# The end of the first channel mixer, done in token halves that follow each other

## The chip, the cores and the metric

The kernel runs on one core of a Trainium2 chip. The metric is the device time of one execution in microseconds (us). Three runs took 3246.5, 3255.47 and 3258.47 us, median 3255.47 us. The profiled execution is one more, of 3260.19 us.

Engines are named as in the profile: PE does the matrix products, DVE, ACT and POOL work elementwise on tiles of 128 partitions, SP issues most of the DMAs. Each engine has a queue of its own, and its instructions start in the trace in the order of that queue.

## The reference

A sequence of 1024 tokens with 1024 features, after 16 meta tokens, goes through two blocks. What matters here is the end of the first block, its channel mixer, and the start of the second, in the parts of a recurrent mixer (RWKV) that are projections with a token shift:

```
y = (gelu(conv(rmsnorm(x1, g_pre) @ w_gate)) * (rmsnorm(x1, g_pre) @ w_up)) @ w_down
x2 = x1 + rmsnorm(y, g_post)                     # end of the first block
p = rmsnorm(x2, mix_norm_gain) @ w_in            # second block
p = p + (shift(p) - p) * mix                     # shift: one token back
r, k, v, wd, ad, gd = split(p)                   # 512 columns each for r, k, v
w = w0 + tanh(wd) @ w_lora_up;  a = sigmoid(a0 + ad @ a_lora_up);  g = sigmoid(gd) @ g_lora_up
kk = normalised k * k_k, per head                # "removal"
```

The columns of wd, ad and gd are the "lora" columns: 128 of them in a first projection (l1) and 32 in a second (l2).

## The kernel before, in words

Activations lie with features on partitions: eight tiles (j = 0 to 7) of 128 features by 1024 tokens, worked on in two token halves, columns 0 to 511 and 512 to 1023. Every product is made of three fp32r products (`mm3`, L196 to L198): high by high, high by low and low by high part. So each operand is split: the high part by a rounding copy on ACT, the low part by a subtraction on DVE or POOL.

**The down projection** (`down`) sums over 22 hidden tiles, taken two at a time. For a pair it loads hidden tile and weights and splits both (four tiles `dn` of each tag XH and XL, which hold eight each, so two pairs are there at once). Then for the first token half, and then for the second, and for each j, six matmuls of 512 columns sum the pair in a PSUM bank, and DVE adds the bank to `y` (L149). On the last pair, `each` also feeds the first norm: ACT squares `y`, POOL adds the squares of j = 0 to 6 in `acc`, and PE sums `acc` and the last square over the partitions (`add_sums`, L292, four matmuls of one column that the trace shows as eight records).

**The end of the mixer** (`ffn1`) then makes the inverse root from the sums (`rstd`: thirteen tiny DVE operations, the wide `rdg`, and four PE matmuls at L318 that spread it over the partitions). For each half and each j: a scaling of `y` (DVE, L156), the residual `x1` loaded from DRAM and added (POOL, L149), the high part `xh` (ACT) and the low part `xl` (DVE, L156), the square for the second norm (ACT, and L292 on PE), and a store of the result to `dx2`. A second `rstd` per half gives `rs`, by which later projections are scaled.

**The second block** begins with the weights of the lora products, then `lora_in`: `shifted` for l1, then for l2, each over both token halves: a weight column of `w_in`, 24 matmuls for each half, `p` (DVE, the PSUM bank times `rs`), a difference on POOL and a combination `d` on DVE. Its results go through tanh to DRAM (`dlora`), from where later steps read them. Then come rotary tables, the attention mask, the output gate (bank q), and the twelve projections r, k, v (`rkv`), the four k first (key0 to key3), each of these followed by `removal`: a square on ACT, two matmuls into the one bank c1 (`pc`), logarithm and exponential on ACT, and a chain over DVE and POOL whose scratch tiles lie in tag A, which holds three. In this region two PSUM banks (m0, m1) take the projections.

The order in every engine's queue is fixed when the program is built: a scheduler replays the program with its own durations and places each instruction where it would be free to go. The order of the source is its wish, not its result.

Of the kernel before, what the change touches and what calls it, by code (L numbers as in the profile page):

```python
# [8 lines left out]
F32 = mybir.dt.float32  # L9
# [8 lines left out]
P = 128  # L18
D = 1024
KD = 8  # L20
# [28 lines left out]
class Build:  # L49
# [1102 lines left out]
    def down(self, hid, w_down, y, last, each=None, after=None, between=None):  # L1152
# [14 lines left out]
        for f in range(0, NF, 2):  # L1167
            fs = [load(f), load(f + 1)]
            end = f == NF - 2
            for a, b in last if end else CH2:  # L1170
                for j in range(KD):
                    ps = self.mm_ps([P, b - a])
                    for i, (g, w) in enumerate(fs):
                        self.mm3(ps, (w[0][:, j, :], w[1][:, j, :]), (g[0][:, a:b], g[1][:, a:b]), i == 0, i == 1)
                    if f == 0:
                        nc.scalar.copy(y[j][:, a:b], ps)
                    else:
                        self.tt(y[j][:, a:b], y[j][:, a:b], ps, ALU.add)
                    if each and end:
                        each(j, a, b)  # L1180
                if after and end:
                    after(a, b)
            if between:
                between(f)

    def ffn1(self, fx):
# [18 lines left out]
        self.down(hid, I["w_ffn_down"][0], y, CH2, each)  # L1205
        rp = [self.rstd(tot[a], b - a, D) for a, b in CH2]
        self.rs = self.slot([P, T2], name="rs", tag="R")
        self.xh, self.xl = [], []
        for i, (a, b) in enumerate(CH2):
            tot = self.sums_ps()  # L1210
            for j in range(KD):
                if j % 2 == 0:
                    x1 = self.slot([P, 2, b - a], name="x1", tag="XE")
                    self.dma(out=x1, in_=self.dx1[j:j + 2, :, a:b].rearrange("j p t -> p j t"))
                if i == 0:
                    self.xh.append(self.slot([P, T2], F32R, "xh", "XH"))
                    self.xl.append(self.slot([P, T2], F32R, "xl", "XL"))
                h, l = self.xh[j][:, a:b], self.xl[j][:, a:b]
                t = y[j][:, a:b]
                self.stt(t, t, gp[:, j:j + 1], rp[i], ALU.mult, ALU.mult)  # L1220
                self.tt(t, t, x1[:, j % 2], ALU.add, eng=nc.gpsimd)
                self.act(h, t, AF.Copy, scale=gm[:, j:j + 1])
                self.stt(l, t, gm[:, j:j + 1], h.bitcast(F32), ALU.mult, ALU.subtract)
# [933 lines left out]
```

## Time and profile before

| | |
|---|---|
| median of three runs | 3255.47 us |
| the profiled execution | 3260.19 us |
| its span in the trace | 3258.5 us |
| PE busy | 3022.7 us, 93% |
| DVE / POOL / ACT busy | 62% / 41% / 35% |
| mean granted TensorE clock | 0.939 |

The last matmul of the down projection starts at 1592.87 us of the span and key0 starts at 1658.37 us. The clock that PE was granted is given as a share of the full 2.4 GHz; 0.50 is 1.2 GHz. A matmul that waits for another engine leaves the queue standing; a wait is listed with the engine that ended it. The slower half of a stretch may be due to the clock as well as to waits, so the granted clock stands in each row of a stretch.

### The profile page before, as it was taken

To read this page: it belongs to the slowest core of one execution; us is meant where nothing else is said; L and a number is where in the kernel's file an instruction comes from. 1 tells how busy PE (TensorE), PEld (TensorE's weight loads), DVE (VectorE), ACT (ScalarE), POOL (GpSimd) and SP (SyncE) were. 2 spreads that over 40 slices of the span, in tenths; PEclk is the share of its full clock that TensorE was granted. 3 is DMA by queue.
4 is the path that set the end of the run, shared out by engine and by line. 5 is a ranking of instruction groups with operands and counts; after the bars stand their busy time and mean duration, and the time that the engine had idled before them with its cause. 6 is when DMAs were issued, how large, how long until landed. Compare 5 with 4: busy or idle time off the path is not lost.

```text
span 3258.5 us, 52664 instructions
## 1 busy us (share of the span) xinstructions
PE 3022.7 (93%) x20614; PEld 2686.7 (82%) x20614; DVE 2010.1 (62%) x3618; ACT 1138.8 (35%) x2166; POOL 1337.7 (41%) x1291
## 2 busy tenths in 40 slices
PE   7999999989889999999999988977998899999998
PEld 6899999879789999877877776766787788887777
DVE  6555653774676666466766555557665866664666
ACT  3334323334343333311333323334444433334111
POOL 2777310033664444232532355542204754454430
PEclk9999999889799999999899988858998899999999
DMA  5233631335212222432223554443336122224321
GB/s 132 84 99 102 180 108 47 99 105 144 83 53 84 79 83 81 155 103 73 91 86 134 147 129 113 111 114 109 100 102 207 52 78 84 78 78 170 120 84 52
DMA packets 322535, 336.83 MB, mean 103 GB/s; under 512 B 60081, under 2 KB 270734, under 8 KB 322286
## 3 DMA queue, kind: packets, MB, share of 16 engines
q1 hardware_dynamic: 289168, 310.22, 30.6%
q10 hardware_dynamic: 33118, 23.24, 2.4%
q8 instruction: 162, 2.65, 0.3%
q14 instruction: 87, 0.71, 0.1%
HBM read 232.66 MB, written 96.40 MB: 101 GB/s over the span
## 4 chain that ended last, share of the span: by engine, by line
PE 62%; DVE 11%; POOL 5%; issue 5%; DMA 5%; ACT 2%; SPq 1%; ACTq 0%; DVEq 0%; POOLq 0%
PE pm L196 13%; PE pm L197 13%; PE pm L198 12%; PE px L197 5%; PE px L196 5%; PE px L198 5%; DVE dn L149 2%; PE px L292 1%; POOL Z L149 1%; POOL fs L149 1%; DVE t L149 1%; PE pa L1856 1%; PE pc L1523 1%; SPq L142 1%; DVE y L149 1%
## 5 line engine op out<-in xcount | busy, mean ns | idle before, releaser
L196 PE MATMUL pm<-xh,whi 128*128 128x512 f32 (+5 forms) x1344 | 453.1, 337 | 17.4 <-DVE th L149 14.2
L198 PE MATMUL pm<-xh,wlo 128*128 128x512 f32 (+5 forms) x1344 | 451.4, 336 | 1.0 <-DVE wlo L149 1.0
L197 PE MATMUL pm<-xl,whi 128*128 128x512 f32 (+5 forms) x1344 | 451.9, 336 | 0.0
L149 DVE TENSOR_TENSOR y<-y,pm 128x512 f32<-128x512 f32 (+1 forms) x336 | 218.0, 659 | 159.9 <-PE pm L198 159.6
L196 PEld LDWEIGHTS pm<-xh,whi 128*128 128x128 f32 (+1 forms) x1344 | 261.4, 194 | 40.3 <-DVE th L149 12.5
L196 PE MATMUL pm<-dn,dn 128*128 128x512 f32 (+1 forms) x736 | 285.8, 389 | 6.9 <-DVE y L149 6.4
L197 PE MATMUL pm<-dn,dn 128*128 128x512 f32 (+1 forms) x736 | 282.7, 384 | 0.7 <-POOL dn L149 0.7
L198 PE MATMUL pm<-dn,dn 128*128 128x512 f32 (+1 forms) x736 | 282.6, 384 | 0.0
L198 PEld LDWEIGHTS pm<-xh,wlo 128*128 128x128 f32 (+1 forms) x1344 | 260.8, 194 | 22.0 <-DVE wlo L149 1.4
L197 PEld LDWEIGHTS pm<-xl,whi 128*128 128x128 f32 (+1 forms) x1344 | 261.4, 195 | 19.5 <-issue 0.5
L149 POOL TENSOR_TENSOR dn<-hid,dn 128x1024 fp32r<-128x1024 f32 x44 | 131.7, 3011 | 250.9 <-ACT dn L1160 250.9
L197 PE MATMUL px<-t,sh 128*128 128x258 f32 (+2 forms) x684 | 218.0, 319 | 7.4 <-DVE t L149 7.4
L196 PE MATMUL px<-t,sh 128*128 128x258 f32 (+2 forms) x684 | 216.9, 317 | 1.4 <-DVE gt L149 1.3
L198 PE MATMUL px<-t,sl 128*128 128x258 f32 (+2 forms) x684 | 215.9, 316 | 0.0
L149 DVE TENSOR_TENSOR wlo<-wraw,whi 128x1024 fp32r<-128x1024 f32 (+2 forms) x114 | 157.6, 1384 | 86.3 <-ACT whi L170 80.2
L196 PEld LDWEIGHTS pm<-dn,dn 128*128 128x128 f32 x736 | 138.2, 188 | 44.3 <-DVE y L149 14.4
L170 ACT CAST whi<-wraw 128x1024 fp32r<-128x1024 f32 (+2 forms) x114 | 103.3, 907 | 184.5 <-PE pm L197 153.8
L198 PEld LDWEIGHTS pm<-dn,dn 128*128 128x128 f32 x736 | 138.2, 188 | 29.9
L197 PEld LDWEIGHTS pm<-dn,dn 128*128 128x128 f32 x736 | 138.4, 188 | 29.6 <-POOL dn L149 1.2
L170 ACT CAST dn<-wd 128x1024 fp32r<-128x1024 f32 x44 | 46.1, 1047 | 291.2 <-PE pm L197 290.7
L149 POOL TENSOR_TENSOR wraw<-wraw,par 128x1024 f32<-128x1024 f32 (+1 forms) x36 | 76.0, 2111 | 173.1 <-DMA wraw<-in_w_in_dram 137.5
L197 PEld LDWEIGHTS px<-t,sh 128*128 128x128 f32 x684 | 130.7, 191 | 18.2 <-DVE t L149 9.4
(611 smaller groups left out, 8771.1 us busy)
## 6 DMA issues: line engine op xcount, KB each, us to landing
wraw<-in_w_in_dram SPq DMA_DIRECT2D x61, 512.0 KB
dhid<-up SPq DMA_DIRECT2D x44, 512.0 KB
wd<-in_w_ffn_down_dram SPq DMA_DIRECT2D x44, 512.0 KB
hid<-dhid SPq DMA_DIRECT2D x44, 512.0 KB
wra<-in_w_ffn_up_dram SPq DMA_DIRECT2D x33, 512.0 KB
wrb<-in_w_ffn_up_dram SPq DMA_DIRECT2D x33, 512.0 KB
dg<-th SPq DMA_DIRECT2D x16, 514.0 KB
wraw<-in_w_out_dram SPq DMA_DIRECT2D x16, 512.0 KB
```

What stands on the lines that cost most here:

```text
L142: self.nc.sync.dma_start(out=out, in_=in_)
L149: (eng or self.nc.vector).tensor_tensor(out=o, in0=a, in1=b, op=op)
L170: self.nc.scalar.copy(hi, src)
L196: nc.tensor.matmul(ps, a[0], b[0], start=start, stop=False, **kw)
L197: nc.tensor.matmul(ps, a[0], b[1], start=False, stop=False, **kw)
L198: nc.tensor.matmul(ps, a[1], b[0], start=False, stop=stop, **kw)
L292: self.nc.tensor.matmul(ps[:bw, i:i + 1], src[:, i * bw:i * bw + bw], self.ones[:, 0:1], start=start and i == 0, stop=stop and i == n - 1)
L1523: nc.tensor.matmul(ps[:, h], maps[c][:, h], S[:, h], start=True, stop=True)
L1856: nc.tensor.matmul(self.po[:, i - 4 * ch], pT[:, i * P - a:i * P - a + P], self.vx[j % 2][:, k].rearrange("p e v -> p (e v)")[:, 2 * e:2 * ...
```

## The change

`down` gets a helper `chunk`, and where `each` is given (the first mixer) the last four hidden tiles are kept together: first token half with the first pair, first token half with the second pair, and then the second half with all four in one sum of twelve matmuls per j. The first half's norm, scaling, residual and second sum (`update`, with the residual added by DVE in place of POOL) are written inside `down`, in front of the second half. The splits of the first half come behind `down`, since all XH and XL tiles are taken until its last matmuls; then come the second half's norm, update and split. `shifted` takes several specifications: l1, l2 and key0 are projected together, their three first halves and then their three second halves. The tiles p and d of l1 and l2 lie in tag A and those of key0 in T, the weights of l2 in a small `narrow` tile (tag W). `lora_in` comes ahead of `lora_weights`, and `rkv` takes key0 ready made. Of the diff the new lines stand here; those taken out, but for the residual's add, are in the functions printed above.

```diff
...
+        def chunk(fs, a, b, first, end):
+            for j in range(KD):
+                ps = self.mm_ps([P, b - a])
+                for i, (g, w) in enumerate(fs):
+                    self.mm3(ps, (w[0][:, j, :], w[1][:, j, :]), (g[0][:, a:b], g[1][:, a:b]), i == 0, i == len(fs) - 1)
+                if first:
+                    nc.scalar.copy(y[j][:, a:b], ps)
+                else:
+                    self.tt(y[j][:, a:b], y[j][:, a:b], ps, ALU.add)
+                if each and end:
+                    each(j, a, b)
+            if after and end:
+                after(a, b)
+        joint = 4 if each else 0
+        for f in range(0, NF - joint, 2):
...
+                chunk(fs, a, b, f == 0, end)
...
+        if joint:
+            (a, b), *others = last
+            fs = [load(f) for f in (NF - 4, NF - 3)]
+            chunk(fs, a, b, False, False)
+            more = [load(f) for f in (NF - 2, NF - 1)]
+            chunk(more, a, b, False, True)
+            for a, b in others:
+                chunk(fs + more, a, b, False, True)
...
+        def update(j, a, b, rp, x1, ps):
+            t = y[j][:, a:b]
+            self.stt(t, t, gp[:, j:j + 1], rp, ALU.mult, ALU.mult)
+            self.tt(t, t, x1[:, j % 2], ALU.add)
+            self.square_sum(ps, t, j == 0, j == KD - 1)
+            self.dma(out=self.dx2[j, :, a:b], in_=t)
+        def residual(j, a, b):
+            x1 = self.slot([P, 2, b - a], name="x1", tag="XE")
+            self.dma(out=x1, in_=self.dx1[j:j + 2, :, a:b].rearrange("j p t -> p j t"))
+            return x1
+        def split(j, a, b):
+            h, l, t = self.xh[j][:, a:b], self.xl[j][:, a:b], y[j][:, a:b]
+            self.act(h, t, AF.Copy, scale=gm[:, j:j + 1])
+            self.stt(l, t, gm[:, j:j + 1], h.bitcast(F32), ALU.mult, ALU.subtract)
+        def after(a, b):
+            if a:
+                return
+            rp, ps = self.rstd(tot[a], b - a, D), self.sums_ps()
...
-                self.tt(t, t, x1[:, j % 2], ALU.add, eng=nc.gpsimd)
...
+                    x1 = residual(j, a, b)
+                update(j, a, b, rp, x1, ps)
+            self.rstd(ps, b - a, D, self.rs[:, a:b])
+        self.down(hid, I["w_ffn_down"][0], y, CH2, each, after)
+        self.xh, self.xl = ([self.slot([P, T2], F32R, n, t) for _ in range(KD)] for n, t in (("xh", "XH"), ("xl", "XL")))
+        (a, b), (c, d) = CH2
+        for j in range(KD):
+            split(j, a, b)
+        rp, ps = self.rstd(tot[c], d - c, D), self.sums_ps()
+        for j in range(KD):
+            if j % 2 == 0:
+                x1 = residual(j, c, d)
+            update(j, c, d, rp, x1, ps)
+            split(j, c, d)
+        self.rstd(ps, d - c, D, self.rs[:, c:d])
...
+    def shifted(self, *specs):
+        ws, pp, res = [], [], []
+        for j0, m, _, tag in specs:
+            ws.append(self.wcol(self.I["w_in_2"][0], j0, m) if m == P else self.narrow(self.I["w_in_2"][0], j0, m))
+            pp.append(self.slot([P, T2 + 1], name="p", tag=tag)[:m])
+        for c in CH2:
+            for (j0, m, _, _), w, p in zip(specs, ws, pp):
+                self.proj(w, self.x, [c], lambda ci, a, b, ps: self.tt(p[:, 1 + a:1 + b], ps, self.rs[:m, a:b], ALU.mult), m=m)
+        for (j0, m, mix, tag), p in zip(specs, pp):
+            self.ts(p[:, :1], p[:, 1:2], 0.0, ALU.mult)
+            d = self.slot([P, T2], name="d", tag=tag)[:m]
+            self.tt(d, p[:, :T2], p[:, 1:], ALU.subtract, eng=self.nc.gpsimd)
+            self.stt(d, d, mix, p[:, 1:], ALU.mult, ALU.add)
+            res.append(d)
+        return res
+    def narrow(self, src, c0, m):
+        raw, hi, lo = (self.slot([P, KD, m], dt, "nw", "W") for dt in (F32, F32R, F32R))
+        self.dma(out=raw, in_=src[:, c0:c0 + m].rearrange("(k p) m -> p k m", p=P))
+        self.split_to(hi, lo, raw)
+        return hi, lo
...
+        l1, l2, self.key0 = self.shifted((1536, P, self.par["mix_lora"][:, 0:1], "A"), (1664, 32, self.mixl[:, 0:1], "A"),
+                                         (512, P, self.par["mix"][:, 4:5], "T"))
...
+                if (i, j) == (1, 0):
+                    t = self.key0
+                else:
+                    t, = self.shifted((512 * i + j * P, P, self.par["mix"][:, 4 * i + j:4 * i + j + 1], "T"))
...
+        B.lora_in()
```

What the schedule made of it stands in the order of the queues. In these rows a number behind a name is that of the buffer.

On PE, around l1 in the program before (`pm_2127` and `pm_2128` are the halves of l1, `px_2098` the sums of the second half's second norm, `px_2097` the spread inverse root):

```order
10172 L197 MATMUL pm_2128_16457<-xl_16116,whi_16426 128x512
10173 L198 MATMUL pm_2128_16457<-xh_16115,wlo_16427 128x512
10174 L196 MATMUL pm_2128_16457<-xh_16128,whi_16426 128x512
10175 L197 MATMUL pm_2128_16457<-xl_16129,whi_16426 128x512
10176 L198 MATMUL pm_2128_16457<-xh_16128,wlo_16427 128x512
10177 L292 MATMUL px_2098_16249<-ones_71,sq_16304 128x1 x4
10178 L292 MATMUL px_2098_16249<-ones_71,sq_16315 128x1 x4
10179 L292 MATMUL px_2098_16249<-ones_71,sq_16328 128x1 x4
10180 L318 MATMUL px_2097_16243<-rdg_16241,ones_71 128x128 x4
10181 L292 MATMUL px_2098_16249<-ones_71,sq_16339 128x1 x4
10182 L196 MATMUL pm_2128_16457<-xh_16143,whi_16426 128x512
```

On PE in the changed program, from the end of l1's first half (`pm_2123`) on (`px_2068` the sums of the second half's first norm, `px_2089` its spread root, `px_2090` the sums of its second norm, `pm_2125` key0's and `pm_2124` l2's first half):

```order
10162 L198 MATMUL pm_2123_16413<-xh_16185,wlo_16395 128x512
10163 L292 MATMUL px_2068_16167<-ones_71,acc_14331 128x1 x4
10164 L292 MATMUL px_2068_16167<-ones_71,sq_16172 128x1 x2
10165 L318 MATMUL px_2053_16030<-rdg_16028,ones_71 128x128 x4
10166 L292 MATMUL px_2068_16167<-ones_71,sq_16172 128x1 x2
10167 L318 MATMUL px_2089_16228<-rdg_16226,ones_71 128x128 x4
10168 L292 MATMUL px_2090_16233<-ones_71,sq_16238 128x1 x4
...
10175 L292 MATMUL px_2090_16233<-ones_71,sq_16321 128x1 x4
10176 L196 MATMUL pm_2125_16465<-xh_16178,whi_16408 128x512
...
10182 L196 MATMUL pm_2124_16439<-xh_16178,nw_16400 32x512
```

Before, the matmuls of l1's second half stand between these sums; now all of l1's first half stands ahead of the second half's two norms, and the first halves of key0 and l2 behind both of them. The spread root of the first half's first norm stands 21 matmuls ahead of the end of the down projection.

On ACT in the program before, where the down projection ends (the squares of the second half's first norm, then the first split and the first square of the second norm):

```order
1086 L159 ACTIVATE sq_16032<-y_14328 128x512
1087 L159 ACTIVATE sq_16043<-y_14329 128x512
1088 L159 ACTIVATE sq_16059<-y_14330 128x512
1089 L159 ACTIVATE xh_16115<-y_14323,par_117 128x512
1090 L159 ACTIVATE sq_16121<-y_14323 128x512
```

On ACT in the changed program (up to row 1097 the first half's second norm and split, from 1098 on the squares of the second half's first norm):

```order
1094 L159 ACTIVATE sq_15996<-y_14329 128x512
1095 L159 ACTIVATE xh_16184<-y_14329,par_117 128x512
1096 L159 ACTIVATE sq_16005<-y_14330 128x512
1097 L159 ACTIVATE xh_16185<-y_14330,par_117 128x512
1098 L159 ACTIVATE sq_16065<-y_14324 128x512
1099 L159 ACTIVATE sq_16082<-y_14325 128x512
...
1104 L159 ACTIVATE sq_16172<-y_14330 128x512
```

The squares of the second half's first norm stood ahead of every split; now they stand behind the splits and squares of the first half. On DVE, too, the first half's scalings, adds and splits stand ahead of the second half's first norm, and `p` of l1's first half stands behind all of the second half's scalings, adds and splits.

On PE in the program before, the first two removals (`pc`, two each) with other matmuls between them:

```order
10374 L1361 MATMUL pc_2189_16783<-rm_16779,blk_16386 128x512
10375 L1677 MATMUL pq_2151_16625<-ident_66,mask_16601 128x128 x4
...
10396 L1361 MATMUL pc_2190_16786<-rm_16779,blk_16386 128x512
10397 L196 MATMUL pq_2158_16649<-gd_16646,lg_16640 128x512
...
10473 L1361 MATMUL pc_2201_16865<-rm_16861,blk_16386 128x512
10474 L196 MATMUL pq_2168_16683<-gd_16680,lg_16640 128x512
```

And in the changed program:

```order
10464 L1410 MATMUL pc_2182_16770<-rm_16763,blk_16370 128x512
10465 L196 MATMUL pq_2157_16696<-gd_16693,lg_16687 128x512
...
10506 L1410 MATMUL pc_2193_16849<-rm_16845,blk_16370 128x512
...
10513 L1410 MATMUL pc_2194_16852<-rm_16845,blk_16370 128x512
...
10568 L1410 MATMUL pc_2205_16931<-rm_16927,blk_16370 128x512
10569 L1410 MATMUL pc_2206_16934<-rm_16927,blk_16370 128x512
```

From the second `pc` of the first removal to the first `pc` of the second there were 77 rows and are 42; from there to the third removal there are 55 (70 before, rows 10498 to 10568).

## Rows read from the trace of the kernel before

**Rows 1.** The page: busy time by engine.
```profile
PE 3022.7 (93%) x20614; PEld 2686.7 (82%) x20614; DVE 2010.1 (62%) x3618; ACT 1138.8 (35%) x2166; POOL 1337.7 (41%) x1291
```
**Rows 2.** Windows: stretch, length, busy PE, PEld, DVE, ACT, POOL, clock, DMA, GB/s.
```profile
1600.00:1610.00 10.00, 10.00 (x39) 9.13 (x40) 9.83 (x17) 6.97 (x12) 7.98 (x6) 0.50 0.99 327
...
1640.00:1650.00 10.00, 10.00 (x38) 7.12 (x38) 7.38 (x36) 1.63 (x2) 0.41 (x1) 0.74 0.02 6
1650.00:1660.00 10.00, 10.00 (x44) 5.29 (x43) 7.17 (x17) 4.83 (x6) 6.09 (x9) 1.00 0.31 102
1660.00:1680.00 20.00, 20.00 (x89) 16.27 (x88) 17.01 (x21) 5.85 (x9) 7.63 (x2) 1.00 0.27 76
...
1840.00:2200.00 360.00, 309.80 (x3771) 261.09 (x3770) 192.11 (x445) 120.78 (x265) 191.94 (x546) 0.81 0.47 119
```
**Rows 3.** Timeline of PE: start, duration, engine, line, operation, count, idle before.
```profile
1592.87 0.40 PE L198 MATMUL pm<-dn,dn 128*128 128x512 f32 x1
...
1604.19 1.70 PE L292 MATMUL px<-ones,sq 128*128 128x1 f32 x8
...
1612.75 2.08 PE L318 MATMUL px<-rdg,ones 128*128 128x128 f32 x8
...
1640.13 0.63 PE L197 MATMUL pm<-xl,whi 128*128 128x512 f32 x1
1640.56 0.63 PE L198 MATMUL pm<-xh,wlo 128*128 128x512 f32 x1
...
1647.18 0.48 PE L196 MATMUL pm<-xh,whi 128*32 128x512 f32 x1
...
1658.37 0.39 PE L196 MATMUL pm<-xh,whi 128*128 128x512 f32 x1
```
**Rows 4.** Timeline of DVE, the two scalings and the last inverse root.
```profile
1594.98 5.36 DVE L156 SCALAR_TENSOR_TENSOR y<-y,par,px 128x512 f32<-128x512 f32 x8 [0.73 <-ACT sq L159]
...
1614.86 5.36 DVE L156 SCALAR_TENSOR_TENSOR y<-y,par,px 128x512 f32<-128x512 f32 x8 [2.17 <-PE px L318]
...
1639.73 0.38 DVE L153 TENSOR_SCALAR px<-px 128x4 f32<-128x4 f32 x2 [5.30 <-PE px L292]
...
1642.49 0.69 DVE L149 TENSOR_TENSOR rdg<-ident,px 128x512 f32<-128x512 f32 x1
1643.10 0.69 DVE L149 TENSOR_TENSOR p<-pm,rs 128x512 f32<-128x512 f32 x1
```
**Rows 5.** Timeline of POOL: last hidden tiles, squares of the first norm, residuals.
```profile
1547.52 6.30 POOL L149 TENSOR_TENSOR dn<-hid,dn 128x1024 fp32r<-128x1024 f32 x2 [17.19 <-ACT dn L1160]
...
1590.69 4.03 POOL L149 TENSOR_TENSOR acc<-acc,sq 128x512 f32<-128x512 f32 x3 [3.29 <-ACT sq L159]
...
1615.69 11.72 POOL L149 TENSOR_TENSOR y<-y,x 128x512 f32<-128x512 f32 x8 [7.71 <-DVE y L156]
```
**Rows 6.** Timeline of ACT: a split and a square; two weight casts.
```profile
1533.37 1.05 ACT L170 CAST whi<-wraw 128x1024 fp32r<-128x1024 f32 x1 [7.50 <-DMA wraw<-in_w_in_dram]
1538.07 0.41 ACT L170 CAST whi<-wraw 128x256 fp32r<-128x256 f32 x1 [3.65 <-DMA wraw<-in_w_in_dram]
...
1598.82 0.72 ACT L159 ACTIVATE xh<-y,par 128x512 fp32r<-128x512 f32 x1
1599.44 0.61 ACT L159 ACTIVATE sq<-y 128x512 f32<-128x512 f32 x1
```
**Rows 7.** Timeline around the first and second removal.
```profile
1695.16 1.02 PE L1361 MATMUL pc<-rm,blk 128*128 128x512 f32 x2
1696.22 0.69 DVE L153 TENSOR_SCALAR rm<-pc 128x512 f32<-128x512 f32 x1 [4.24 <-PE pc L1361]
...
1711.14 1.06 ACT L159 ACTIVATE rm<-rm 128x1024 f32<-128x1024 f32 x1 [6.21 <-DVE rm L153]
...
1713.65 1.02 PE L1361 MATMUL pc<-rm,blk 128*128 128x512 f32 x2
```
**Rows 8.** Waits of PE from 1645 to 1840: for whom, us in total, times, longest.
```profile
PE pm L196 <- DVE p L149: 3.1, 2, 1.7
```

More of the change, by code (lines that the diff above doesn't have):

```diff
@@ L1165, in load @@
             return (gh, gl), (wh, wl)
-        for f in range(0, NF, 2):
+        def chunk(fs, a, b, first, end):
[13 more added lines that the diff above has]
+        for f in range(0, NF - joint, 2):
             fs = [load(f), load(f + 1)]
@@ L1170, in down @@
             for a, b in last if end else CH2:
[L1171 to L1182, printed above, removed]
+                chunk(fs, a, b, f == 0, end)
             if between:
                 between(f)
+        if joint:
[6 more added lines that the diff above has]
+                chunk(fs + more, a, b, False, True)
     def ffn1(self, fx):
@@ L1203, in each @@
             self.square_sum(tot[a], y[j][:, a:b], False, True)
-        self.down(hid, I["w_ffn_down"][0], y, CH2, each)
-        rp = [self.rstd(tot[a], b - a, D) for a, b in CH2]
         self.rs = self.slot([P, T2], name="rs", tag="R")
-        self.xh, self.xl = [], []
-        for i, (a, b) in enumerate(CH2):
-            tot = self.sums_ps()
+        def update(j, a, b, rp, x1, ps):
[4 more added lines that the diff above has]
+            self.dma(out=self.dx2[j, :, a:b], in_=t)
@@ L1211, in ffn1 @@
             for j in range(KD):
                 if j % 2 == 0:
[L1213 to L1219, printed above, removed]
@@ L1220, in ffn1 @@
-                self.stt(t, t, gp[:, j:j + 1], rp[i], ALU.mult, ALU.mult)
-                self.tt(t, t, x1[:, j % 2], ALU.add, eng=nc.gpsimd)
-                self.act(h, t, AF.Copy, scale=gm[:, j:j + 1])
-                self.stt(l, t, gm[:, j:j + 1], h.bitcast(F32), ALU.mult, ALU.subtract)
-                self.square_sum(tot, t, j == 0, j == KD - 1)
-                self.dma(out=self.dx2[j, :, a:b], in_=t)
-            self.rstd(tot, b - a, D, self.rs[:, a:b])
+                    x1 = residual(j, a, b)
@@ L1294, in out_gate @@
                 self.dma(out=self.dbon[j, :, 1, a:b], in_=t)
-    def shifted(self, j0, m, mix):
-        w = self.wcol(self.I["w_in_2"][0], j0, m)
-        p = self.slot([P, T2 + 1], name="p", tag="T")[:m]
-        self.proj(w, self.x, CH2, lambda ci, a, b, ps: self.tt(p[:, 1 + a:1 + b], ps, self.rs[:m, a:b], ALU.mult), m=m)
-        self.ts(p[:, :1], p[:, 1:2], 0.0, ALU.mult)
-        d = self.slot([P, T2], name="d", tag="T")[:m]
-        self.tt(d, p[:, :T2], p[:, 1:], ALU.subtract, eng=self.nc.gpsimd)
-        self.stt(d, d, mix, p[:, 1:], ALU.mult, ALU.add)
-        return d
+    def shifted(self, *specs):
[18 more added lines that the diff above has]
+        return hi, lo
     def lora_in(self):
         self.dlora = self.dram([160, T2], "dlora")
-        l1 = self.shifted(1536, P, self.par["mix_lora"][:, 0:1])
+        l1, l2, self.key0 = self.shifted((1536, P, self.par["mix_lora"][:, 0:1], "A"), (1664, 32, self.mixl[:, 0:1], "A"),
+                                         (512, P, self.par["mix"][:, 4:5], "T"))
         self.act(l1[:32], l1[:32], AF.Tanh)
@@ L1313, in lora_in @@
         self.dma(out=self.dlora[:P], in_=l1)
-        l2 = self.shifted(1664, 32, self.mixl[:, 0:1])
         self.act(l2, l2, AF.Tanh, scale=0.5)
@@ L2078, in block2 @@
         B.constants2()
+        B.lora_in()
         B.lora_weights()
-        B.lora_in()
         B.rotary_tables()
```

1 line of the change is left out of this document (removed).

## The prediction

> **What bounds the kernel now.** The page says first that PE is busy 93% of the span [rows 1]. A share over the whole span says little about one place, so I went on to the windows around the end of the mixer [rows 2]. There PE counts as busy all the time and yet does little: from 1600 to 1610 it runs at a granted clock of 0.50, in 39 records, while 1650 to 1660 at 1.00 holds dense work. The timeline of PE gives the ends of this stretch [rows 3]. The last matmul of the down projection ends at 1592.87 + 0.40 = 1593.3; call this E. Key0 starts at 1658.37 and has 48 matmuls. The matmuls of l2, also 48, take 1658.37 - 1647.18 = 11.2 us, which is 0.233 us for one; so key0 ends at 1669.6, E + 76.3. The 144 matmuls of l1, l2 and key0 would be 33.6 us at that pace. So some 43 us between E and E + 76.3 go to the norms and the slow clock, and these are what the change is about. What fills them shows on the other engines: two scalings of 5.36 us at 1594.98 and 1614.86 [rows 4], residuals of 11.72 us on POOL [rows 5], and the inverse root at 1639.73. After 1660 PE is full again (20.00 of 20) [rows 2]: what comes late here comes late there.
>
> **The change, part by part.** I follow the queues of the changed program from E to the end of key0, and then look at what lies behind.
>
> *Up to E, nothing.* The down projection has its 192 matmuls for the last four tiles either way. The eight adds into `y` that the joint sums save lie on DVE under twelve matmuls each (2.8 us against about 0.6). The second pair is wanted earlier: its first matmul stands 146 rows ahead of the end, at about E - 33. Its last split on POOL ends at 1547.52 + 6.30 = 1553.8, E - 39.5 [rows 5]; that covers it by 6 us. The spread of the first half's inverse root (L318) now stands among the matmuls, so E comes about 1.0 later (2.08 us at half the clock [rows 3], halved).
>
> *First half.* L318 stands 21 matmuls (4.9 us) ahead of that end, so DVE has the factor at E + 1.0 - 4.9 = E - 3.9. Eight scalings take 5.36 [rows 4], to E + 1.5. Then come ten adds and eight splits `xl`. An add of 128x512 with two SBUF inputs is not in this stretch on DVE. Between `rdg` at 1642.49 and the next DVE row lie 0.61 us [rows 4], and POOL took 1.46 for it (11.72 / 8 [rows 5]). I take 0.62, the row of the same engine and shape, and keep 1.46 as the other end. A split costs a scaling's 0.67. So 10 x 0.62 + 8 x 0.67 = 11.6, to E + 13.1. ACT goes along with a square and a split per j, 1.23 us (the square starts 0.62 after the split and takes 0.61 [rows 6]), and is done at about E + 12. Only a small part of this lies ahead of E; most of it does not hide.
>
> *Second half, first norm.* Its seven squares stand on ACT behind the last `xh`. So they start at E + 12, although their `y` are ready at about E. POOL follows at E + 12.6 with six adds of 1.34 (4.03 / 3 [rows 5]): 8.1, to E + 20.7. PE then has two sums of 1.70 and a spread of 2.08 [rows 3]: E + 26.2. The inverse root takes 1643.10 - 1639.73 = 3.4 [rows 4], its spread 2.1: E + 31.7. Before, this root was made beside the first half's scalings and its spread stood at 1612.75, E + 19.5. This is the step in which the change loses most.
>
> *Second half, second norm.* Scalings to E + 37.1; the first add and square to E + 38.3. Eight sums of 1.70 follow on PE, 13.6: E + 51.9. DVE is done sooner: 37.1 + 8 x 0.62 + 8 x 0.67 + 0.6 for `p` = E + 48. That `p` empties bank m1 for key0. The last residual is loaded behind two stores; a load of this size is 4.7 us by the distance of the casts at 1533.37 and 1538.07 [rows 6], which leaves DVE waiting about 2 us and still under E + 51.9.
>
> *Projections.* Behind these sums stand the first halves of key0 and l2 and all second halves, 120 matmuls: 28.0 us at 0.233. From 1640 to 1650 the mean clock was 0.74 with matmuls back to back, hence 5.2 us at 0.50 [rows 2]; a matmul took 0.43 there (1640.56 - 1640.13 [rows 3]). So about 13 matmuls cost 0.19 more, 2.5 us; with one spread of 1.0 this makes 31.5, and key0 ends at E + 83.4. The narrow weights of l2 are now loaded behind the stores, at about E + 46; with 4.7 for the load and 0.8 for two casts they are there at E + 51.5, and their first matmul stands six behind key0's start, at E + 54. That cover is thin, but it holds.
>
> **Term A: 83.4 - 76.3 = +7.** Lower bound: sums and spreads of these norms at full clock give back 3.8 (until `p` sets the end instead) and 3.7, so about 0. Upper bound: DVE adds at POOL's 1.46, which puts DVE's splits at E + 64 and key0's end 12 later, +19.
>
> What lets 48 matmuls wait here is the queue. In the trace of before PE stood with the same sums between its matmuls, and the row at 1604.19 comes where the order has it [rows 3]. The Trainium skill, page "PSUM — Partial Sum Buffer", section "Engine vs sequencer instructions", says that matmuls start and complete in program order and that the queues of the other three are strict first in, first out. By that rule the first halves of key0 and l2 cannot slip ahead of the sums, and term A stands; could they slip, their 48 matmuls would fill the gap and key0 would end some 11 us sooner.
>
> **Term B: +2.** From 1660 to 1680 DVE was busy 17.01 of 20 us [rows 2]. In the changed program the lora results and the rotary steps come later and meet the k projections on DVE and POOL. Then `p` is late and a projection finds no bank. The nearest rows are two such waits of 3.1 us in all, the longest 1.7 [rows 8]. I take 2, bounds 0 and 3.
>
> **Term C: +9.** The removals now stand closer together, since key0 comes early and l1 and l2 no longer lie between. From the second `pc` at 1695.16 its result is read at 1696.22; the square of the next removal ends at 1711.14 + 1.06 = 1712.2 [rows 7]. That chain took 16.0 us; I allow up to 2 us of it for other work that stood in it, so 14 to 16. Before, 77 rows lay in this distance, 17.9 us at 0.233, and the next `pc` came at 1713.65. Now 42 rows lie there, 9.8 us: PE waits 4.3 to 6.2. For the third removal there are 55 rows, 12.8 us: 1.3 to 3.2. Where two `pc` stand side by side and share the bank, PE waits for the read between, about 1.0 each, once or twice. Sum 6.6 to 11; I take 9.
>
> **Term D: 0.** From 1840 to 2200 PE is busy 309.80 of 360 us [rows 2]. The 50 us of idle time there could swallow what came late, if what ends those waits is done earlier by the clock of the program; or the late lora results could lengthen them. No row decides it. The bounds are -15 and +15, about the terms in front of it.
>
> **Sum.** 7 + 2 + 9 + 0 = +18. The profiled execution was 3260.2 us, so its like would be 3278; that execution lies 4.7 above the median of the runs shown, 3255.5. Against the median I predict 3274.
>
> **The rivals.**
>
> *The overlap works (faster).* If the first half's norm, scalings and splits were done under the joint matmuls (22 us) and the second half's first norm did not queue behind them, the stretch would lose one of its two rounds: 1614.86 - 1594.98 = 19.9 us [rows 4], so 3236. For it: half of the work is offered 22 us earlier, and POOL's 23 us of residuals go from the path. Against it: ACT's squares stand behind the splits, and L318 only 21 matmuls ahead of E. It decides when the second half's spread root comes before E + 20, where it stood before, in place of E + 31.7.
>
> *Swallowed (no change).* The stretch is late by 18, and the idle 50 us behind 1840 take it: 3255 to 3262. For it: the chains there run on POOL and DMA and partly start from early projections. Against it: PE is full up to 1840, so all projections end late.
>
> *More than that (slower).* The adds cost DVE what they cost POOL (+12 in term A), or the late lora results add their 15 in term D: 3286 to 3289. Against it: DVE's 128x512 rows are all 0.6 to 0.7 when alone.
>
> *It does not do what it says.* This is in the forecast: the halves follow each other in the source, yet the queues put only l1's first half ahead of the second half's norms.
>
> **How the numbers follow.** I give the forecast 0.50, the overlap 0.15, the swallowing 0.20, the larger loss 0.15. A measurement of this kernel can tell 0.5%, 16 us, from no change: below 3239 is faster, above 3272 slower. The forecast's own range is 3262 to 3287; by its centre at 3274 some 0.35 of 0.50 lies above 3272. Slower: 0.35 + 0.15 + a little of the swallowing = 0.52. Faster: most of the overlap, 0.12. The rest, 0.36, is the same. The range runs from 3240 to 3300: it leaves out the overlap's better half and a loss where the upper bounds of A and D add up.
>
> **What would show it.** In the changed profile the stretch from the last `dn` matmul to the end of key0 is to be 80 to 88 us (76.3 before); ACT's squares of the second half begin about 12 us behind E; the second half's scalings start near E + 32 (1614.86, E + 21.6, before); PE's clock is 0.50 through most of the gap; `pc` waits on ACT `rm` appear among PE's waits with 6 to 10 us. I am wrong if the scalings start before E + 20, if key0 ends within 76 us of E, or if the time lost up to the removals is gone again at the last third of the program.

## The result, and the profile after

The changed kernel takes 3278.9 us (median of 6, 3276.7 to 3286.4), the kernel before 3255.5 (median of 6 beside it, 3240.9 to 3263.0). The ratio is 1.0082 [1.0064, 1.0100]: 27 us slower by the ratio, 23 by the medians. The profiled execution of the changed kernel took 3277.2 us, 1.7 below its median, that of before 4.7 above its own; so the two traces differ by 17 us only, and the traces are compared with each other, the medians with each other.

The page's busy times of the changed kernel stand beside [rows 1]: PE and ACT hardly move, and the residuals have gone from POOL to DVE.

```profile
PE 3030.4 (93%) x20614; PEld 2691.9 (82%) x20614; DVE 2003.6 (61%) x3626; ACT 1137.1 (35%) x2165; POOL 1309.5 (40%) x1275
```

Below, E' is the end of the last matmul of the down projection in the kernel that is looked at: 1595.93 + 0.40 = 1596.3 after, E = 1593.3 before. T0, the first matmul of that projection, is at 1336.1 and 1334.4; so E' is 1.3 us late, counted from T0. (T0 lies ahead of the change, and between 1333.4 and 1338.8 in the fourteen traces: by so much single executions, or their layouts, differ before anything of this stretch begins.) PE's timeline of the changed kernel (start, us, engine, line, operation; in brackets the idle time before, and what ended it) answers to [rows 3]:

```profile
1590.38 1.05 PE L318 MATMUL px<-rdg,ones 128*128 128x128 f32 x8
1595.93 0.40 PE L198 MATMUL pm<-dn,dn 128*128 128x512 f32 x1
1627.08 2.05 PE L318 MATMUL px<-rdg,ones 128*128 128x128 f32 x8 [3.63 <-DVE rdg L149]
1635.84 13.81 PE L292 MATMUL px<-ones,sq 128*128 128x1 f32 x64 [6.71 <-ACT sq L159]
1649.52 0.77 PE L196 MATMUL pm<-xh,whi 128*128 128x512 f32 x1
1706.20 0.47 PE L196 MATMUL pm<-xh,whi 128*128 128x512 f32 x1 [3.65 <-DVE p L149]
1740.73 2.08 PE L1410 MATMUL pc<-rm,blk 128*128 128x512 f32 x2 [5.10 <-ACT rm L159]
1759.92 1.12 PE L1410 MATMUL pc<-rm,blk 128*128 128x512 f32 x2 [1.06 <-ACT rm L159]
1762.72 2.07 PE L1410 MATMUL pc<-rm,blk 128*128 128x512 f32 x2 [1.68 <-DVE rm L153]
```

The eight sums are one block of 64 records that PE starts at 1635.84, and the key projections go on right behind it. The 144th matmul of l1, l2 and key0 ends at E' + 83.7 (before: E + 76.4, counted in the same way). From there to the last transposes of v (`pc<-ident,d`) it is 170.5 us, before 157.4. That is the whole loss up to this place: 1.3 + 7.3 + 13.1 = 21.7 us. The waits of PE in this second stretch are, by engine, line and releaser (us in total, times, longest), first after:

```profile
PE pc L1410 <- ACT rm L159: 6.2, 2, 5.1
PE pm L196 <- DVE p L149: 3.7, 1, 3.7
PE pc L1410 <- DVE rm L153: 1.7, 1, 1.7
```

and before, besides [rows 8], one more:

```profile
PE pc L1348 <- DVE d L156: 0.9, 1, 0.9
```

11.6 us against 4.0. The rest of the 13.1 is slower matmuls: PE's busy time, 5.8 us longer. This stands in windows (us, then busy time and records of PE, PEld, DVE, ACT, POOL, then clock, DMA share, GB/s), answering to [rows 2]. The stretch from key0's end to the last transposes as a whole, and pieces behind its waits, after:

```profile
1680.00:1850.90 170.90, 159.41 (x673) 124.33 (x672) 101.41 (x132) 55.12 (x72) 43.58 (x24) 0.96 0.38 123
1704.00:1707.00 3.00, 0.80 (x4) 0.70 (x5) 3.00 (x4) 0.00 (x0) 0.00 (x0) 1.00 0.42 175
1707.00:1710.00 3.00, 3.00 (x10) 2.40 (x9) 3.00 (x6) 0.00 (x0) 0.00 (x0) 0.61 0.00 0
1740.00:1743.00 3.00, 2.27 (x3) 1.17 (x4) 2.84 (x2) 1.19 (x2) 2.81 (x1) 0.50 0.56 196
1743.00:1746.00 3.00, 3.00 (x9) 1.64 (x7) 3.00 (x5) 1.09 (x2) 0.00 (x0) 0.63 0.61 206
1764.00:1767.00 3.00, 3.00 (x10) 2.09 (x10) 1.66 (x4) 1.31 (x2) 1.26 (x1) 0.72 0.68 199
```

and the same stretch before:

```profile
1669.70:1827.40 157.70, 153.63 (x672) 121.71 (x671) 96.44 (x107) 51.34 (x65) 41.72 (x16) 1.00 0.40 131
```

PE needs 159.41 us for what took 153.63, with one record more. Behind the longer waits its clock is 0.5 to 0.7 for some microseconds, and 9 or 10 matmuls fit into 3 us where e6 below has 15 at 1.00. DVE on the changed kernel, at the end of the mixer ([rows 4] before) and around the late `p`:

```profile
1591.55 5.36 DVE L156 SCALAR_TENSOR_TENSOR y<-y,par,px 128x512 f32<-128x512 f32 x8 [0.98 <-PE px L318]
1596.83 1.29 DVE L149 TENSOR_TENSOR y<-y,x 128x512 f32<-128x512 f32 x2
1629.17 5.36 DVE L156 SCALAR_TENSOR_TENSOR y<-y,par,px 128x512 f32<-128x512 f32 x8 [2.23 <-PE px L318]
1634.44 3.69 DVE L149 TENSOR_TENSOR y<-y,x 128x512 f32<-128x512 f32 x6
1699.06 2.79 DVE L156 SCALAR_TENSOR_TENSOR e<-f,e 128x1024 f32<-128x1024 f32 x1
1701.89 1.23 DVE L149 TENSOR_TENSOR c<-c,e 128x1024 f32<-128x1024 f32 x1
1704.23 1.22 DVE L156 SCALAR_TENSOR_TENSOR c<-f,c 128x1024 f32<-128x1024 f32 x1
1705.37 0.68 DVE L149 TENSOR_TENSOR p<-pm,rs 128x512 f32<-128x512 f32 x1
```

The adds stand behind all eight scalings, not between them. The `p` for which PE waits 3.65 us stands behind 1024-wide steps of the attention mask (tiles c, e, f), 5.2 us of them in the rows shown, and one 1024-wide combination `d` between them. ACT's squares at the end of the mixer ([rows 6] before):

```profile
1597.61 0.63 ACT L159 ACTIVATE sq<-y 128x512 f32<-128x512 f32 x1 [22.06 <-DVE y L149]
1608.68 0.63 ACT L159 ACTIVATE sq<-y 128x512 f32<-128x512 f32 x1 [1.75 <-PE px L292]
1635.16 0.63 ACT L159 ACTIVATE sq<-y 128x512 f32<-128x512 f32 x1 [11.43 <-DVE y L149]
```

The first square of the first half waits for the first add. The second half's squares of the first norm begin at E' + 12.4 (row 1608.68), and its scalings at E' + 32.8 (before E + 21.6).

### The profile page after: what moved, and what is told of

It is laid out like the page before. It is cut to its first block, busy times and chain, and to the rows that moved or that the text cites. A ratio compares the mean times of both kernels' runs of the same rounds, so it can differ in the third digit from the quotient of the medians.

```text
span 3275.5 us, 52673 instructions
## 1 busy us (share of the span) xinstructions
PE 3030.4 (93%) x20614; PEld 2691.9 (82%) x20614; DVE 2003.6 (61%) x3626; ACT 1137.1 (35%) x2165; POOL 1309.5 (40%) x1275
## 4 chain that ended last, share of the span: by engine, by line
PE 63%; DVE 11%; issue 5%; POOL 5%; DMA 4%; ACT 2%; SPq 1%; ACTq 0%; DVEq 0%; POOLq 0%
PE pm L196 13%; PE pm L197 13%; PE pm L198 12%; PE px L197 5%; PE px L196 5%; PE px L198 5%; DVE dn L149 2%; PE px L292 2%; POOL Z L149 1%; POOL fs L149 1%; PE pc L1572 1%; PE pa L1905 1%; DVE t L149 1%; SPq L142 1%; PE pc L1652 1%
## 5 line engine op out<-in xcount | busy, mean ns | idle before, releaser
L196 PE MATMUL pm<-xh,whi 128*128 128x512 f32 (+4 forms) x1328 | 444.6, 335 | 18.0 <-DVE th L149 14.4
L197 PE MATMUL pm<-xl,whi 128*128 128x512 f32 (+4 forms) x1328 | 445.4, 335 | 0.0
L198 PE MATMUL pm<-xh,wlo 128*128 128x512 f32 (+4 forms) x1328 | 443.7, 334 | 1.0 <-DVE wlo L149 1.0
L196 PEld LDWEIGHTS pm<-xh,whi 128*128 128x128 f32 x1328 | 258.8, 195 | 39.1 <-DVE th L149 12.7
L198 PEld LDWEIGHTS pm<-xh,wlo 128*128 128x128 f32 x1328 | 259.0, 195 | 19.4 <-DVE wlo L149 1.3
L197 PEld LDWEIGHTS pm<-xl,whi 128*128 128x128 f32 x1328 | 258.7, 195 | 18.4 <-issue 0.7
L149 DVE TENSOR_TENSOR wlo<-wraw,whi 128x1024 fp32r<-128x1024 f32 (+2 forms) x113 | 150.1, 1330 | 86.3 <-ACT whi L170 84.3
```

Of the source, the lines that this page charges most:

```text
L149: (eng or self.nc.vector).tensor_tensor(out=o, in0=a, in1=b, op=op)
L196: nc.tensor.matmul(ps, a[0], b[0], start=start, stop=False, **kw)
L197: nc.tensor.matmul(ps, a[0], b[1], start=False, stop=False, **kw)
L198: nc.tensor.matmul(ps, a[1], b[0], start=False, stop=stop, **kw)
```

## The experiments

A study of twelve kernels, each timed beside the kernel before, whose median in these sessions was 3253.1, 3254.3 and 3255.9; so kernels are compared by the ratio. "Scalings" is the start of the second half's scalings and "key0" the end of the 144th matmul, both behind E'; "stretch" is key0's end to the last transposes. Cuts of code are shown against the changed kernel.

| kernel | median | ratio [95%] | scalings | key0 | stretch |
|---|---|---|---|---|---|
| before | 3255.5 | | 21.6 | 76.4 | 157.4 |
| after | 3278.9 | 1.0082 [1.0064, 1.0100] | 32.8 | 83.7 | 170.5 |
| e1_joint | 3263.6 | 1.0029 [1.0016, 1.0043] | 31.4 | 84.1 | 157.9 |
| e2_group | 3274.7 | 1.0062 [1.0041, 1.0084] | 21.7 | 74.7 | 173.4 |
| e3_pool | 3272.5 | 1.0059 [1.0040, 1.0079] | 27.9 | 75.9 | 171.7 |
| e4_sq2 | 3283.6 | 1.0094 [1.0077, 1.0112] | 32.7 | 86.0 | 175.1 |
| e5_joint_pool | 3268.2 | 1.0043 [1.0025, 1.0062] | 27.6 | 75.8 | 157.2 |
| e6_rk | 3273.5 | 1.0064 [1.0038, 1.0089] | 31.5 | 82.5 | 166.4 |
| e7_acc2 | 3274.0 | 1.0059 [1.0038, 1.0080] | 30.2 | 84.7 | 175.6 |
| e8_joint_acc2 | 3271.1 | 1.0056 [1.0036, 1.0077] | 30.1 | 88.7 | 159.5 |
| e10_mask | 3280.2 | 1.0079 [1.0061, 1.0098] | 31.5 | 82.7 | 152.2 |
| e11_dve | 3263.0 | 1.0023 [1.0009, 1.0036] | 29.0 | 83.1 | 158.0 |
| e12_mask_pool | 3262.3 | 1.0024 [1.0012, 1.0035] | 27.6 | 74.3 | 152.2 |
| e13_before_mask | 3269.3 | 1.0047 [1.0029, 1.0065] | 21.6 | 76.4 | 151.8 |

**Each half of the change alone.** e1 keeps the joint end of the mixer and has the projections as before; e2 is the reverse.

```diff
-        l1, l2, self.key0 = self.shifted((1536, P, self.par["mix_lora"][:, 0:1], "A"), (1664, 32, self.mixl[:, 0:1], "A"),
...
+        l1 = self.shifted(1536, P, self.par["mix_lora"][:, 0:1])
...
+        l2 = self.shifted(1664, 32, self.mixl[:, 0:1])
```

> The joint end of the down projection alone; l1, l2 and key0 are projected one after the other, as before the change. Theory Q (the queues): the second half's norm stands behind the first half's scalings, splits and sums, which costs about 9 us up to the end of key0; the removals keep their old distance of 77 rows and cost nothing more. So 7 to 12 us above the kernel before, and the second half's scalings start about 33 us after the last matmul of the down projection (21.6 before). Rival G (the grouping alone makes the loss): within 3 us of the kernel before.

```diff
-        joint = 4 if each else 0
-        for f in range(0, NF - joint, 2):
+        for f in range(0, NF, 2):
...
+        self.down(hid, I["w_ffn_down"][0], y, CH2, each)
+        rp = [self.rstd(tot[a], b - a, D) for a, b in CH2]
```

> The grouping of l1, l2 and key0 alone, on the old end of the down projection with the residual on POOL. Theory Q: the scalings start 21 to 22 us after the last matmul of the down projection as before, l1's second half moves behind the norm (24 matmuls, 4 to 6 us at the end of key0), and the closer removals cost about 8: 10 to 15 us above the kernel before. Rival G: the whole loss is here, 20 to 25 us above.

e1 costs 9 us and e2 20 us by their ratios, and the change with both 27: within the intervals they add up. e1 came out as theory Q had it; e2 came out where rival G put it, though the whole loss is not there. In the traces key0's delay belongs to e1 alone (84.1 against 74.7), the longer stretch to e2 alone (173.4 against 157.9).

**The residual's add.** e3 is the changed kernel with the add on POOL, e5 is e1 with it, e11 the kernel before with the add on DVE.

```diff
-            self.tt(t, t, x1[:, j % 2], ALU.add)
+            self.tt(t, t, x1[:, j % 2], ALU.add, eng=nc.gpsimd)
```

> The changed kernel with the residual added on POOL as before the change. Theory Q: eight adds take 11.7 us there in place of 5, twice in a row on the way to the end of key0, so 5 to 12 us above the changed kernel. Rival P (the adds moved to DVE are what makes the stretch late): 5 to 10 us below the changed kernel.

> The joint end alone (projections in the old order), with the residual added on POOL. If the two effects seen so far are separate, the joint end with its +9.4 and POOL's adds with -7.5 make about +2 (-2 to +5) against the kernel before, and the second half's scalings start 27 to 28 us after the last matmul of the down projection. If POOL's adds help only where the projections are grouped: +7 to +10 as with DVE's adds.

> The kernel before, with the residual added on DVE in place of POOL, and nothing else. If DVE's adds are late because they stand behind all eight scalings of a half, while POOL's run beside the scalings: the first half's adds begin some 5 us later, in both halves, and key0 ends 6 to 11 us later than the 76.4 us after the last matmul of the down projection. If the adds cost only in the joint end: within 2 us of 76.4.

I expected e3 to be slower by 5 to 12 us, and it came out as its rival P. DVE, POOL and ACT of e3 (E' = 1624.76 - 27.9 = 1596.9):

```profile
1592.13 5.36 DVE L156 SCALAR_TENSOR_TENSOR y<-y,par,px 128x512 f32<-128x512 f32 x8 [0.99 <-PE px L318]
1624.76 5.35 DVE L156 SCALAR_TENSOR_TENSOR y<-y,par,px 128x512 f32<-128x512 f32 x8 [2.03 <-PE px L318]
```

```profile
1592.96 11.33 POOL L149 TENSOR_TENSOR y<-y,x 128x512 f32<-128x512 f32 x8 [18.21 <-DVE y L156]
```

```profile
1594.29 0.63 ACT L159 ACTIVATE sq<-y 128x512 f32<-128x512 f32 x1 [18.12 <-POOL y L149]
```

POOL adds 0.83 us after the first scaling started, beside the other seven. The first square starts 2.2 us behind the start of the scalings, on DVE 6.1 (1597.61 - 1591.55). The second half's scalings come 4.9 us sooner and key0 ends 7.8 sooner, although an add takes POOL 1.42 (11.33 / 8) and DVE 0.62 (3.69 / 6). The time is 7.5 us lower by the ratios, and their intervals overlap. e5 says the same of e1 in the trace (75.8, before 76.4: the joint end as such neither gains nor loses there), but not in time: 8 us less than e1 was expected, and it is 5 us more by the ratios, with intervals that overlap. e11 has the reverse sign, as expected: key0 6.7 us later (6 to 11 expected), and 7.5 in time, 3 to 12 by the interval. A fourth pair follows below, e12 against e10: key0 8.4 us sooner and the time 18 us lower, the intervals clear of each other. So the place of the adds is shown for the end of key0, in four pairs of kernels; in time two of the four show it beyond their intervals.

**The order on ACT, and the second norm's sums.** e4 gives the squares of the second norm buffers of their own. e7 sums them on POOL, so that PE has one sum of two parts in place of eight; e8 is e1 with e7's sums.

```diff
-            self.square_sum(ps, t, j == 0, j == KD - 1)
+            sq = self.slot([P, 512], name="sq", tag="WU")
+            self.act(sq, t, AF.Square)
+            self.add_sums(ps, sq, j == 0, j == KD - 1)
```

> The changed kernel, with tiles of their own (two of tag WU) for the squares of the second norms, so that the second half's first squares no longer wait for buffers that the first half's second squares hold. On ACT they then stand ahead of the first half's splits. If ACT's order is what makes the second norm late: scalings start 8 to 12 us sooner and the kernel is 8 to 12 us below the changed one. If PE's own cold sums and l1's matmuls, which stand ahead of the spread of that root, are the next limit: scalings within 3 us of the changed kernel, and the time 0 to 3 us below it.

```diff
+        acc2 = self.slot([P, T2], name="acc", tag="WU")
...
+                if j < KD - 1:
+                    self.tt(acc2[:, a:b], acc2[:, a:b], sq, ALU.add, eng=nc.gpsimd)
+                else:
+                    self.add_sums(ps, acc2[:, a:b], True, False)
+                    self.add_sums(ps, sq, False, True)
```

> The changed kernel with the squares of the second norms added up on POOL, in tiles of their own, and summed on PE once for each half (16 records in place of 64). If PE's own slow sums hold back the second half (the limit that the run with separate squares left): scalings start 8 to 11 us sooner after the last matmul of the down projection (32.8 in the changed kernel), key0 as much, and the kernel is 8 to 12 us below the changed one. If DVE's chain holds it: scalings and time within 3 us.

> The joint end alone, projections in the old order, with the second norms' squares added up on POOL and summed once. If sums on PE and the closeness of the removals are the whole loss of the change, this is 8 to 12 us below the joint end alone, so -3 to +2 against the kernel before. If the joint end gains something of its own once these are gone: 5 us or more below the kernel before.

None moves key0 forward: 86.0 and 84.7 for 83.7, and in e8 88.7 for the 84.1 of e1. e4 does with ACT's order what it was made for. POOL's last addition of the second half's squares, and what DVE then waits for, are

```profile
1598.13 1.67 POOL L149 TENSOR_TENSOR acc<-acc,sq 128x512 f32<-128x512 f32 x1 [7.90 <-ACT sq L159]
```

```profile
1619.20 0.38 DVE L153 TENSOR_SCALAR px<-px 128x4 f32<-128x4 f32 x2 [11.24 <-PE px L292]
```

So these squares are added up at E' + 5.9 (E' = 1593.9 in e4), where the changed kernel has them at E' + 21.8:

```profile
1611.41 6.75 POOL L149 TENSOR_TENSOR acc<-acc,sq 128x512 f32<-128x512 f32 x5 [0.74 <-ACT sq L159]
```

Yet the scalings start at E' + 32.7, as in the changed kernel. In e4 DVE makes this root together with that of the first half's second norm, whose sums stand on PE among the matmuls of l1 and end at 1619.2. Behind ACT's order lies another wait as long; this was the second of the two outcomes named for e4.

In e7 the eight sums go, and a wait comes in their place, in PE's timeline:

```profile
1603.89 1.86 PE L292 MATMUL px<-ones,acc 128*128 128x1 f32 x8 [4.65 <-POOL acc L149]
1644.98 1.87 PE L292 MATMUL px<-ones,acc 128*128 128x1 f32 x8 [18.54 <-POOL acc L149]
```

The wait of 18.54 us is longer than the 13.81 of sums that went. In this form the chain over DVE, ACT and the new additions on POOL is as long as PE's sums were, and key0 gains nothing; whether the sums cost something where POOL adds nothing new is not shown. By the ratios e7 lies 7.5 us below the changed kernel, with intervals that overlap. That is as much as e3, though key0 is later in e7 and earlier in e3: at this size the time does not tell what key0 gained. e8 lies 9 us above e1, where 8 to 12 below was expected.

**The stretch behind key0.** e6 puts an r projection between any two k projections, so that the removals stand farther apart. e10 leaves the order and moves the attention mask behind r, k and v; e13 does so in the kernel before, as a control; e12 is e10 with the add on POOL.

```diff
-        for i in (1, 0, 2):
-            for j in range(4):
+        for i, j in [(i, j) for j in range(4) for i in (1, 0)] + [(2, j) for j in range(4)]:
```

> The changed kernel with an r projection between every two k projections, so that some 75 rows of PE lie between a removal's last pc and the next removal's first. If the closeness of the removals costs what the waits of PE on their squares and on their bank show (6.2 and 1.7 us in the changed kernel): these waits vanish and the kernel is 6 to 9 us below the changed one. If that time is swallowed behind 1840 us anyway: within 3 us of the changed kernel.

```diff
-        B.attn_mask()
...
+        B.attn_mask()
```

> The changed kernel with the attention mask built behind the r, k and v projections in place of ahead of them. In the changed kernel its 1024-wide steps stand on DVE ahead of p of key1, where PE then waits 3.7 us for a bank, and they push the first removal towards the second. If the mask is what makes the grouping dear: PE's waits on p, on the removals' squares and on their bank (11.6 us) go to 4 or less, PE's clock stays at 1.00 from key0's end to the last transposes of v, and that stretch shrinks from 170.9 us to 158 (157.7 before the change); the kernel is 8 to 14 us below the changed one. If the lora results and the rotary steps are what crowd DVE: the stretch stays above 165.

> The changed kernel with both edits: the residual on POOL and the mask behind the projections. If these two are the whole loss of the change: key0 ends 75 to 77 us after the last matmul of the down projection, the stretch from there to the last transposes takes 158 us, and the kernel lies within 5 us of the kernel before. If the joint end or the grouping loses something of its own: 8 us or more above it.

> The kernel before with the attention mask built behind the projections, as a control. If the mask's steps cost mainly because the grouping moved the k projections onto them: only the 3.1 us of waits on p can go, so 0 to 4 us below the kernel before. If the mask costs the same in the old order: 8 to 14 us below.

In e6 no `pc` wait is left, the stretch is 166.4, the time 6 us below the changed kernel by the ratios (intervals overlap), and PE waits for `p` all the more:

```profile
PE pm L196 <- DVE p L149: 6.2, 2, 3.6
```

In e10 nearly all goes; the only wait left, and the window of the stretch:

```profile
PE pc L1410 <- ACT rm L159: 0.2, 1, 0.2
```

```profile
1682.20:1834.70 152.50, 152.31 (x664) 121.07 (x663) 99.51 (x120) 51.81 (x65) 41.44 (x25) 1.00 0.42 138
```

152.2 us against 151.8 in the control: with the mask out of the way the new grouping costs nothing there. So the removals were not close because l1 and l2 had left; the mask's steps, on DVE by the rows shown above, held key1's `p` and the first removal back, towards the second. The first `pc`, in the changed kernel and in e10:

```profile
1718.97 1.02 PE L1410 MATMUL pc<-rm,blk 128*128 128x512 f32 x2
```

```profile
1695.69 1.02 PE L1410 MATMUL pc<-rm,blk 128*128 128x512 f32 x2
```

That is 38.9 us behind key0's end in the changed kernel, 13.5 in e10 (19.4 before); and from the first removal's last `pc` to the second removal's first, 42 rows of PE have become 76 (77 before). Yet e10 is no faster than the change, where 8 to 14 us less was expected, for the mask is then late for what follows: counted from T0, e10 is 2.9 us behind the kernel before at the transposes, and 20.0 behind where POOL's wait at the start of the recurrence ends. That wait, in e13 (the same 49.3 in e10):

```profile
POOL fs L149 <- DMA M<-dm: 49.3, 1, 49.3
```

and in the kernel before:

```profile
POOL fs L149 <- DMA M<-dm: 32.3, 1, 32.3
```

The control is 6.6 us ahead of the kernel before at the transposes, 10.5 behind it where this wait ends, and 15 us slower in time (0 to 4 faster was expected). With both causes taken out, e12 is 19 us faster than the changed kernel, the intervals clear of each other: so much of the 27 us is theirs. Against the control it is 7 us faster (the intervals overlap a little); against the kernel before it stays 8 us slower, where within 5 was expected if these two were the whole loss. It has the long wait too (50.0), and in its trace most of it is made up again before the end of the attention; how is not shown. No kernel here beats the one before.

## Why the prediction was right, and where its reasons were not

The time, the sign and the sizes up to the transposes came out: 3274 predicted, 3278.9 measured. That the total fits is in part luck: the two largest terms have the right size for reasons that the runs do not bear out, and in the traces the 4 us that the terms fall short of are given back behind 1840. Step by step:

- **Up to E: +1.0, measured +1.3.** Right: the spread takes 1.05 among matmuls at full clock.
- **Term A: +7, measured 8.6 (1.3 + 7.3); size right, cause wrong.** The times nearly hold, with E' at E + 1.3: squares of the second half at E + 13.7 for E + 12, scalings at E + 34.1 for E + 31.7, eight sums 13.81 for 13.6. But the step named as the one in which the change loses most, the second half's first norm behind ACT's splits, is not what makes key0 late. In e4 its squares no longer stand behind the splits and the scalings are not sooner. In e5 that norm is still 6 us later than before (27.6 against 21.6), and key0 is not late at all: from the scalings to key0's end it takes 48.2 us there and 54.8 before, so the new order gives back behind the norm what it loses up to it. What makes key0 late is the residual add: on DVE it stands behind all eight scalings, on POOL it runs beside them (7.8 us in e3, 8.3 in e5, 8.4 in e12, 6.7 the other way in e11). I had priced it at 0.62 by its length on DVE, which was right to the digit, and not by its place. "POOL's 23 us of residuals go from the path" was counted for the overlap; it was a loss. The rival "more than that" looked at the right operation and again at its duration.
- **That the first halves of key0 and l2 cannot pass the sums: right.** No projection matmul starts between 1635.84 and 1649.52. The Trainium skill's rule that I cited (page "PSUM — Partial Sum Buffer", section "Engine vs sequencer instructions": matmuls start and complete in program order) agrees with this trace.
- **Term B: +2, measured 3.7 of wait on `p` against 3.1 before.** The total hardly moved; as one wait of 3.65 it is more than twice the longest of [rows 8]. The work in front of `p` was not the lora or rotary steps that I named but, for the most part, the mask's: in e10 no wait on `p` is left.
- **Term C: +9, measured 7.9 of `pc` waits against 0.9.** The size held, within the 6.6 to 11. That PE waits where the removals stand 42 and 55 rows apart was right; that they stand so because l1 and l2 have left was not: e10 has the same grouping, 76 rows for the 42, and 0.2 us.
- **Left out of the sum: the clock behind the waits.** 5.8 us of the 13.1. I counted the slow matmuls in term A and forgot them in B and C. Terms B and C together were 11 for 13.1 by luck: the 11 were taken as all new while 4.0 of wait stood there before, and the two errors nearly cancel.
- **Term D: 0, and open.** In the traces it is -5: counted from T0, the 21.7 us at the transposes are 16.6 at the end of the attention and 16.7 at the end of the second mixer's down projection. The sign differs between kernels: e1 goes from +8.5 to +1.6 at the end of the attention, e5 from +0.1 to +7.2. From there on the shift hardly moves, so the difference arises in the recurrence and attention between. The scheduler lays out that part differently in every kernel here, and no run isolates one wait of it. A bound of -15 to +15 was honest; a cause I do not have.
- **The rivals.** The overlap did not come: scalings at E' + 32.8, not before E + 20. Of the swallowing the traces show 5 of 21.7 us, not the whole. What the change says it does, it does only in part, as forecast.

The signs named ahead were seen: 83.7 us to key0's end (80 to 88), `pc` waits on ACT `rm` of 6.2 (6 to 10). The trace up to the transposes is explained by runs; what happens in the recurrence and attention behind it is not. That the ratio says 27 us and the two profiled executions 17 needs no cause: single executions of the kernel before lie up to 22 us apart, and the profiled one lay 4.7 above its median.

## What to carry to other kernels

Price a moved elementwise step by where it will stand in its new queue, not by how long it takes: a step twice as long on an idle engine beside its producer can beat a short one behind the producer's whole batch. When a wait is added on PE, look for slow matmuls behind it and keep room for them in the price: here 5.8 us beside 7.6 of added wait. And before a gap between two steps is blamed on what was taken from between them, look at what else stands on the engine that feeds the later one.

## What was not expected of the hardware

Two things. First, the same split on DVE has two prices. Groups of DVE between the two norms, before (line, operation, shapes, count, busy us, mean ns, idle before) and after:

```profile
L156 DVE SCALAR_TENSOR_TENSOR xl<-y,par,xh 128x512 fp32r<-128x512 f32 x16 | 20.4, 1284 | 0.0
```

```profile
L156 DVE SCALAR_TENSOR_TENSOR xl<-y,par,xh 128x512 fp32r<-128x512 f32 x8 | 5.5, 745 | 0.0
```

Before, POOL adds residuals beside most of these splits; after, it does not. The kernel before has both prices by itself: POOL's adds of the first half end at 1607.97, and the splits on either side of that are

```profile
1596.27 11.70 POOL L149 TENSOR_TENSOR y<-y,x 128x512 f32<-128x512 f32 x8
```

```profile
1605.15 1.68 DVE L156 SCALAR_TENSOR_TENSOR xl<-y,par,xh 128x512 fp32r<-128x512 f32 x1
1608.91 0.74 DVE L156 SCALAR_TENSOR_TENSOR xl<-y,par,xh 128x512 fp32r<-128x512 f32 x1
```

DMA traffic alone is not the reason, for it goes on while the splits are short again (POOL 0.00 and DMA 0.91 in this window):

```profile
1608.00:1611.50 3.50, 3.50 (x17) 3.37 (x16) 3.29 (x13) 1.35 (x2) 0.00 (x0) 0.50 0.91 311
```

A scaling, which reads `y` and a PSUM bank, takes 5.36 for eight with POOL's adds beside it (e3) and without. The Trainium skill, page "SBUF — State Buffer", section "Who interferes with whom", says that a DVE operation with two SBUF inputs contends with a GpSimd operation that reads SBUF, for a port pair that one of them holds for its whole instruction. These rows agree with it (1.68 us beside POOL's adds, 0.74 without); that it is the port is not shown apart from this. The same holds for the choice of engine for the add: on DVE it leaves the splits cheaper, and it is still the slower choice here.

Second, a wait of the same length does not always bring down PE's clock. In the changed kernel 3.65 us of wait at 1706.20 are followed by 0.61 (window 1707 to 1710 above). In e6 the same `p` is waited for just as long, and behind it the clock stays at 1.00:

```profile
1704.67 0.47 PE L196 MATMUL pm<-xh,whi 128*128 128x512 f32 x1 [3.65 <-DVE p L149]
```

```profile
1705.00:1708.00 3.00, 3.00 (x15) 2.43 (x14) 3.00 (x6) 0.00 (x0) 1.61 (x1) 1.00 0.00 0
```

What differs between the two is not settled by these runs.
